# Output projection and MLP of a hybrid encoder layer: token blocks swapped in two tile sets, splits made in line, the mean square applied in mlp_down

## The chip, the core and the metric

The kernel runs on one core of one Trainium2 chip. The metric is the device time of one execution in microseconds (us). Five engines work side by side, each through its own instructions in order: TensorE (PE, matrix products), VectorE (DVE), ScalarE (ACT), GpSimd (POOL) and SyncE (SP, which here only issues transfers). On-chip tiles lie in SBUF; matrix products accumulate in PSUM, in eight tiles of 128 x 512 float32. Semaphores make an instruction wait for what it needs.

## What is computed

One layer over x (1, 2048, 1024) in float32: three token mixers (a chunkwise mLSTM, neighbourhood attention, attention into 256 memory tokens), a gated merge, an output projection into the residual stream, and an MLP. The part that the change touches is the end:

```python
def rmsnorm(x, g):
    xf = x.astype(jnp.float32)
    y = xf * lax.rsqrt(jnp.mean(xf * xf, axis=-1, keepdims=True) + EPS)
    return (y * g.astype(jnp.float32)).astype(x.dtype)
...
    y = (gates[:, :, 0] * (h_m @ w_proj_mlstm)
         + gates[:, :, 1] * (h_na @ w_proj_na)
         + gates[:, :, 2] * (h_mem @ w_proj_mem))
    x = x + y @ w_out

    u = rmsnorm(x, g_ffn) @ w_up
    return x + jnp.square(jax.nn.relu(u)) @ w_down
```

D_MODEL is 1024, D_FF is 4096. The norm's factor 1/sqrt(ms), with ms the mean square of a token plus EPS, goes through the relu, is squared to 1/ms, and so can be applied to the MLP's output: out = x + (1/ms) * (relu(x g w_up)^2 w_down).

## The kernel before

Phases 1 and 2 (norm, input projection, mixers) take the first 1300 us. Phase 3 works on token blocks of 512 in two pairs: blocks 3 and 2, then 1 and 0. In a pair, j = 0 is its first block and j = 1 its second. For each pair it runs merge, out_proj, 16 steps of mlp_up and mlp_down.

**Exact float32 products.** mm3 (L230) makes a product of three matmuls of 128 x 512: high part by high part, high by low, low by high (L235, L236, L237). So each operand is split: ACT copies it into a rounded type (the high part), and DVE subtracts that from the source (the low part).

**merge** writes the merged y of a block in both parts into eight 128 x 512 planes, yT[j]: for block 0 the tile hT, for block 1 the tiles b21 and t4, which both lie in the tile B.

**out_proj** takes w_out in two halves of four output tiles. Before, each half runs block 0's four tiles and then block 1's. A tile: load xC (L1354), 24 matmuls, DVE addition (L1363), store of the result x2 to memory, square on ACT (L1371) and its addition into the sum of squares gbc (L1372), and operands(), which makes the operands of the MLP: sums and differences of the four quarters (two blocks by two halves) as a seven-product scheme needs them, called b11, t1, b22, t2, t3, b21 and t4. less() subtracts both parts of an operand made earlier. Block 1's last quarter can't be split at once, since b21 and t4 are still being read as its yT planes: its four tiles are staged in half of uout (the tile that hT becomes after its last read), and eight jobs split them later, at ticks inside PE's sequence (L1400, L1403, L1411, L1412). inverse(), a job too, takes the mean over channels of gbc by a float32 matmul with ones (L1385), scales it (L1386) and takes the reciprocal (L1387), once for each block.

**mlp_up** is a step of seven products, 84 matmuls, for 256 of the 4096 channels. The sixth product reads b21, the seventh t4. The third goes into the PSUM tile c12, is copied by ACT (L1455), and the fifth accumulates into the same tile. The step squares the relu (L1471) and stores its sums. The up weights' seven operands are split on ACT and DVE by fetch_sums (L184) a step ahead.

**mlp_down** is four sweeps over the seven products; each product is 16 x 12 matmuls into four PSUM tiles. A ring of tiles (six places, in the first pair's last part four and then two, since the places go to the next pair's merge) takes operands loaded by SP (L1510 to L1517) and split by ACT and DVE (L1522, L1523). A product is summed into acc for one or two of four outputs (two blocks by two halves): the first by a copy on ACT (L1559), the next by DVE (L1561). Ahead of an output's last product x2 is loaded (L1535), acc is multiplied by 1/ms (L1537) and x2 added (L1538); behind it the product is multiplied (L1555) and added (L1556), and the result is stored.

**Order.** PE's sequence is that of the code (manual_schedule). The other engines' is set by a scheduler, by the priority at which an instruction is emitted; SOON, LATER and LATER_A shift it. ev() gives 128 x 512 tiles from a pool; an instruction into one waits until its last use is done.

**nsb.** In phase 2, na_scores takes a score tile of 128 x 480 from a pool of three and clears the columns behind the scores with a GpSimd memset (L1097).

Of the kernel before, what the change touches and what calls it, by code (L numbers as in the profile page):

```python
# [22 lines left out]
D = 1024  # L23
# [60 lines left out]
class Body:  # L84
# [995 lines left out]
    def na_scores(self, u, h):  # L1080
# [6 lines left out]
        sb = self.t("nsb", [128, 480], 3)  # L1087
# [5 lines left out]
        nc.vector.reciprocal(rs, sm)  # L1093
        nc.vector.tensor_scalar(sb[:, :nk], sb[:, :nk], rs, None, ALU.mult)
        kp = len(u["kts"]) * 120
        if kp > nk:
            nc.gpsimd.memset(sb[:, nk:kp], 0.0)  # L1097
        return u, h, sb

    def na_transpose(self, u, h, sb):  # L1100
# [166 lines left out]
    def phase_3(self):  # L1267
# [20 lines left out]
        for i in range(0, NB, 2):  # L1288
            pair = order[i:i + 2]
            if i:  # L1290
                self.hT = self.p_h.tile([128, 2, 8, TB], F32R, name="yT", tag="hT", bufs=1)
            yT = [[self.hT[:, l] for l in range(2)], [planes("b21"), planes("t4")]]
            self.ahead = 4
            self.merge(pair, mix, yT)
            self.out_proj(pair, yT, i)

            for q in range(FF // 256):
                self.mlp_up(i // 2, q)
            self.ahead = AHEAD
            self.mlp_down(i // 2, pair, [(b, m) for b, m in zip(order[i + 2:i + 4], mix)])  # L1300
# [36 lines left out]
    def out_proj(self, pair, yT, i):  # L1337

        nc, a = self.nc, self.a
        stage = None
        for half in range(2):
            ws = self.take(4)
            for j, b in enumerate(pair):
                if half and j:
                    self.up_tiles(i)
                    stage = self.uout[1].rearrange("p u i t -> p (u i) t")
                sq = self.gbc[:, j * TB:(j + 1) * TB]  # L1350
                for k, w in enumerate(ws):
                    c = 4 * half + k
                    x = self.ev()
                    nc.sync.dma_start(x, a["xC"][c, :, b * TB:(b + 1) * TB])  # L1354
                    p = self.ps("mm")
                    for n in range(8):
                        self.mm3(p, (w[:, 0, n], w[:, 1, n]), (yT[j][0][:, n], yT[j][1][:, n]), n == 0, n == 7)
                        if n % 2:
                            self.tick()
                    to = x if stage is None else stage[:, k]  # L1360
                    prio = self.tc.cur_priority
                    self.tc.cur_priority = prio - SOON
                    nc.vector.tensor_tensor(to, x, p, ALU.add)  # L1363
                    self.tc.cur_priority += SOON
                    x = to
                    self.store(self.scr["x2"][b][c], x)
                    if c == 0:
                        nc.scalar.activation(sq, x, AF.Square)
                    else:
                        e = self.ev()  # L1370
                        nc.scalar.activation(e, x, AF.Square)  # L1371
                        nc.vector.tensor_tensor(sq, sq, e, ALU.add)  # L1372
                    if stage is None:
                        self.operands(x, half, j, k)
                if half:
                    self.jobs += [None] * (LATER_3 - len(self.jobs) - 1) + [lambda sq=sq: self.inverse(sq)]
        for name in ("b21", "t4"):
            for k in range(4):
                self.jobs.append(lambda name=name, k=k, x=stage[:, k]: self.operands(x, 1, 1, k, name))

    def inverse(self, sq):

        nc = self.nc
        p = self.ps("mm")
        nc.tensor.matmul(p, self.ones, sq, start=True, stop=True)  # L1385
        nc.vector.tensor_scalar(sq, p, 1.0 / D, EPS, ALU.mult, ALU.add)  # L1386
        nc.vector.reciprocal(sq, sq)  # L1387

    def operands(self, x, half, j, k, late=None):
# [5 lines left out]
        f32 = lambda n, l: part(n, l).bitcast(F32)  # L1395

        def split(n, src, scale=None):
            if scale is None:
                nc.scalar.activation(part(n, 0), src, AF.Copy)
                nc.vector.tensor_tensor(part(n, 1), src, f32(n, 0), ALU.subtract)  # L1400
            else:
                nc.scalar.activation(part(n, 0), src, AF.Copy, scale=scale)
                nc.vector.scalar_tensor_tensor(part(n, 1), src, scale, f32(n, 0), ALU.mult, ALU.subtract)  # L1403

        def less(src, n, scale=None):

# [1 line left out]
            if scale is None:  # L1408
                nc.vector.tensor_tensor(e, src, f32(n, 0), ALU.subtract)
            else:  # L1410
                nc.vector.scalar_tensor_tensor(e, src, scale, f32(n, 0), ALU.mult, ALU.subtract)  # L1411
# [72 lines left out]
    def mlp_down(self, i, pair, then):  # L1484
# [43 lines left out]
        for q in range(0, FF // 256, 4):  # L1528
            for _, _, s, more, out in products:
                last = q == FF // 256 - 4 and (out, s, more) in ((0, 1, False), (3, 0, True), (1, 1, True), (2, 0, True))  # L1530
                if last:
                    j, h0 = pair[out // 2], out % 2 * 512
                    r2, xs = self.gbc[:, out // 2 * TB:(out // 2 + 1) * TB], [self.ev() for _ in range(4)]
                    for t, x in enumerate(xs):
                        nc.sync.dma_start(x, self.scr["x2"][j][out % 2 * 4 + t])  # L1535
                        c = acc[:, out, t]
                        nc.vector.tensor_tensor(c, c, r2, ALU.mult)  # L1537
                        nc.vector.tensor_tensor(x, x, c, ALU.add)  # L1538
                for dq in range(4):
                    if dq % 2 == 0:  # L1540
                        while todo and len(ready) < ring(total - len(todo))[1]:
# [9 lines left out]
                                 not more and dq == 0, dq == 3, more)  # L1551
                for t, p in enumerate(sets[s]):
                    c = acc[:, out, t]
                    if last:
                        nc.vector.tensor_tensor(c, p, r2, ALU.mult)  # L1555
                        nc.vector.tensor_tensor(xs[t], xs[t], c, ALU.add)  # L1556
                        self.store(self.a["out"][h0 + t * 128:h0 + t * 128 + 128, j * TB:(j + 1) * TB], xs[t])
                    elif out not in seen:
                        nc.scalar.activation(c, p, AF.Copy)  # L1559
                    else:  # L1560
                        nc.vector.tensor_tensor(c, c, p, ALU.add)  # L1561
                seen.add(out)

            sets.reverse()

# [74 lines left out]
```

## Time and profile before

| | us |
|---|---|
| median of 3 runs (2916.24 to 2921.32) | 2919.31 |
| profiled run, its own time | 2916.24 |
| its span | 2914.5 |
| merge, first and second pair | 87.05, 87.04 |
| out_proj | 88.88, 89.07 |
| 16 up steps | 317.97, 318.14 |
| mlp_down | 314.46, 304.79 |

The span is what the profiler sees of an execution; 1.74 us lie around it. The stage lengths are from PE's instructions of the trace: merge of the first pair from 1300.80 to 1387.85, of the second from 2109.16 to 2196.20; the others are in the rows quoted below. The mean granted clock is 0.993 of full speed. In a timeline a row gives start, length, engine, line, operation, output <- input, shape, and in brackets the idle time ahead of it and what ended it.

### The profile page before, as it was taken

Reading aid. Unit: us, or ns where it says so; the run is one execution under the profiler, and the core shown is the slowest. Engines: PE = TensorE matmul, PEld = TensorE weight load, DVE = VectorE, ACT = ScalarE, POOL = GpSimd, SP = SyncE. Lnnn points to the kernel's source line nnn. Section 1 sums busy time; section 2 is a strip of 40 time slices with the busy share of each in tenths; the row PEclk is TensorE's granted clock in tenths of the full one; section 3 lists DMA queues with packets and bytes.
Section 4 is the critical chain, followed back from the end, with each engine's and each line's share of the span. In section 5 each row is a group of like instructions: output and inputs, shape, how many; then the busy total and the mean of one; then the engine's idle time right before and its main releaser. Section 6 shows DMA issues by size and latency. Waiting matters only on the chain.

```text
span 2914.5 us, 41662 instructions
## 1 busy us (share of the span) xinstructions
PE 2862.8 (98%) x14932; PEld 2361.3 (81%) x14932; DVE 2055.8 (71%) x3494; ACT 1186.9 (41%) x2224; POOL 214.2 (7%) x382
## 2 busy tenths in 40 slices
PE   8999999999999999999989999999999899999999
PEld 6888788878878888888868888888788688888887
DVE  6676865477764556738688887666886888885668
ACT  6464654355543443532333334433223333344332
POOL 4121210021000122300000000000000000000000
PEclk9999999999999999999999999999999999999999
DMA  8786878877898788977344447556763344476554
GB/s 277 228 280 192 245 238 248 261 224 224 272 307 301 253 282 270 311 267 240 105 137 148 149 159 253 210 197 225 276 203 116 123 159 154 150 243 208 192 190 160
DMA packets 345151, 632.24 MB, mean 217 GB/s; under 512 B 29584, under 2 KB 151376, under 8 KB 344944
## 3 DMA queue, kind: packets, MB, share of 16 engines
q1 hardware_dynamic: 344944, 629.58, 66.2%
q8 instruction: 118, 1.93, 0.3%
q14 instruction: 89, 0.73, 0.1%
HBM read 452.85 MB, written 176.62 MB: 216 GB/s over the span
## 4 chain that ended last, share of the span: by engine, by line
PE 77%; DVE 9%; issue 8%; DMA 4%; ACT 1%; SPq 1%; POOL 0%; DVEq 0%; POOLq 0%; ACTq 0%
PE mm L235 24%; PE mm L237 23%; PE mm L236 23%; DMA wr<-in_w_units_dram 1%; PE tr L1105 1%; PE pn L882 1%; DVE ws L180 1%; DMA ev<-in_xC_dram 1%; PE pn L885 1%; PE mx L891 1%; PE mx L1119 1%; PE mx L1086 1%; DVE ev L1412 1%; DVE ev L1411 1%; DMA nak<-s_ks 1%
## 5 line engine op out<-in xcount | busy, mean ns | idle before, releaser
L235 PE MATMUL mm<-X,ws 128*128 128x512 f32 x896 | 352.8, 394 | 0.0
L236 PE MATMUL mm<-X,ws 128*128 128x512 f32 x896 | 351.0, 392 | 0.0
L237 PE MATMUL mm<-X,ws 128*128 128x512 f32 x896 | 350.6, 391 | 0.0
L180 DVE TENSOR_TENSOR ws<-wr,ws 128x1024 fp32r<-128x1024 f32 (+1 forms) x194 | 240.9, 1248 | 127.2 <-ACT ws L179 124.1
L235 PE MATMUL mm<-hT,ws 128*128 128x512 f32 (+1 forms) x776 | 308.9, 398 | 1.3 <-ACT ev L565 0.7
L237 PE MATMUL mm<-hT,ws 128*128 128x512 f32 (+1 forms) x776 | 302.9, 390 | 0.0
L236 PE MATMUL mm<-hT,ws 128*128 128x512 f32 (+1 forms) x776 | 302.5, 390 | 0.0
L179 ACT ACTIVATE ws<-wr 128x1024 fp32r<-128x1024 f32 (+1 forms) x194 | 204.2, 1058 | 116.5 <-PE mm L237 81.7
L237 PE MATMUL mm<-X 128*128 128x512 f32 x616 | 241.1, 391 | 4.8 <-DVE X L1523 4.8
L235 PE MATMUL mm<-X 128*128 128x512 f32 x616 | 241.0, 391 | 1.0 <-ACT X L1522 1.0
L236 PE MATMUL mm<-X 128*128 128x512 f32 x616 | 240.7, 391 | 0.0
L235 PE MATMUL mm<-ws,hT 128*128 128x512 f32 (+2 forms) x640 | 233.1, 364 | 2.9 <-ACT zif L529 2.2
L205 ACT ACTIVATE ws<-wr 128x512 fp32r<-128x512 f32 x224 | 134.5, 628 | 230.0 <-PE mm L237 151.3
L237 PE MATMUL mm<-ws,hT 128*128 128x512 f32 (+2 forms) x640 | 225.1, 352 | 2.0 <-DVE hT L438 2.0
L236 PE MATMUL mm<-ws,hT 128*128 128x512 f32 (+2 forms) x640 | 224.2, 350 | 0.0
L235 PEld LDWEIGHTS mm<-X,ws 128*128 128x128 f32 x896 | 169.8, 189 | 36.4 <-issue 0.8
L236 PEld LDWEIGHTS mm<-X,ws 128*128 128x128 f32 x896 | 169.6, 189 | 36.3 <-issue 1.0
L237 PEld LDWEIGHTS mm<-X,ws 128*128 128x128 f32 x896 | 169.4, 189 | 35.2
L1522 ACT ACTIVATE X<-X 128x1024 fp32r<-128x1024 f32 x109 | 115.7, 1062 | 194.1 <-DMA X<-s_s 93.1
L1523 DVE TENSOR_TENSOR X<-X 128x1024 fp32r<-128x1024 f32 x109 | 132.2, 1223 | 59.7 <-ACT X L1522 58.9
L235 PEld LDWEIGHTS mm<-hT,ws 128*128 128x128 f32 x776 | 146.4, 189 | 32.4 <-issue 4.3
L237 PEld LDWEIGHTS mm<-hT,ws 128*128 128x128 f32 x776 | 146.1, 188 | 31.3
(285 smaller groups left out, 5981.8 us busy)
## 6 DMA issues: line engine op xcount, KB each, us to landing
wr<-in_w_units_dram SPq DMA_DIRECT2D x290, 512.0 KB
s_s<-u SPq DMA_DIRECT2D x32, 1024.0 KB
s_g<-ev SPq DMA_DIRECT2D x96, 256.0 KB
ev<-s_g SPq DMA_DIRECT2D x96, 256.0 KB
s_a<-u SPq DMA_DIRECT2D x96, 256.0 KB
X<-s_s SPq DMA_DIRECT2D x45, 512.0 KB
nab<-in_rpb_dram SPq DMA_DIRECT2D x96, 220.0 KB
xt<-in_w_units_dram SPq DMA_DIRECT2D x32, 512.0 KB
```

The lines of the kernel that those rows point to most:

```text
L179: nc.scalar.activation(w[:, 0], raw, AF.Copy)
L180: nc.vector.tensor_tensor(w[:, 1], raw, w[:, 0].bitcast(F32), ALU.subtract)
L205: nc.scalar.activation(hi, src, AF.Copy)
L235: mm(out, lhs[0], rhs[0], start=first, stop=False)
L236: mm(out, lhs[0], rhs[1], start=False, stop=False)
L237: mm(out, lhs[1], rhs[0], start=False, stop=last)
L882: mm(pn[h % 2][:, h // 2], pt[:, h], v1[:, h], start=h < 2, stop=first)
L885: mm(pn[h % 2][:, h // 2], qw[hp, h // 2], C[hp, h // 2], start=False, stop=True)
L891: nc.tensor.matmul(pu[hp, h // 2], kw[:, h], v1[:, h], start=True, stop=True)
L1086: nc.tensor.matmul(psc[:, :nk], q[:, h, u["half"] * 128:u["half"] * 128 + 128], kl, start=True, stop=True)
L1522: nc.scalar.activation(hi, src, AF.Copy)
L1523: nc.vector.tensor_tensor(lo, src, hi.bitcast(F32), ALU.subtract)
```

## The change

- **Blocks swapped.** Block 0's yT planes are b21 and t4, block 1's are hT. In out_proj's first half the two blocks of a tile follow each other (k outside, j inside); in the second half all of block 0 comes first. So when block 1's last quarter comes, b21 and t4 are free, and its tiles are split at once; the staging and the eight late jobs go, and up_tiles (uout, utmp) is called behind out_proj.
- **t1** is the difference of the two blocks' first halves. Block 0's tile is kept (kept[k]) until block 1's comes, the difference is taken from the two and split once. Before it was made of block 0's operand through less(). 88 in place of 96 DVE operations on tiles in each pair.
- **inverse()** becomes means(), ahead of the third up step (q == 2): both blocks' matmuls with ones and the scaling, with no reciprocal. gbc then holds ms.
- **mlp_down** loads x2 at an output's first product, multiplies it by ms, and adds the first product to it (DVE, no ACT copy); then sums as before. At the last product acc is multiplied by 1/ms and stored. The reciprocals are taken in place in the first sweep, behind the last product that opens an output.
- **nsb**: three tiles cleared once; DVE clears the columns again only for units with g == 7, in which fewer key columns are filled.

```diff
+        self.nsb = [p_a.tile([128, 480], F32, name=f"nsb{i}") for i in range(3)]
+        for x in self.nsb:
+            nc.vector.memset(x, 0.0)
...
-        if kp > nk:
-            nc.gpsimd.memset(sb[:, nk:kp], 0.0)
+        if u["g"] == 7:
+            nc.vector.memset(sb[:, nk:kp], 0.0)
...
-            yT = [[self.hT[:, l] for l in range(2)], [planes("b21"), planes("t4")]]
+            yT = [[planes("b21"), planes("t4")], [self.hT[:, l] for l in range(2)]]
             self.ahead = 4
             self.merge(pair, mix, yT)
-            self.out_proj(pair, yT, i)
-
+            self.out_proj(pair, yT)
+            self.up_tiles(i)
             for q in range(FF // 256):
+                if q == 2:
+                    self.means()
                 self.mlp_up(i // 2, q)
...
         for half in range(2):
             ws = self.take(4)
+            for k, j in [(k, j) for k in range(4) for j in range(2)] if not half else [(k, j) for j in range(2) for k in range(4)]:
+                b, c, w = pair[j], 4 * half + k, ws[k]
...
+                self.operands(x, half, j, k, kept)
+
+    def means(self):
+
+        nc = self.nc
+        for j in range(2):
+            sq = self.gbc[:, j * TB:(j + 1) * TB]
+            p = self.ps("mm")
+            nc.tensor.matmul(p, self.ones, sq, start=True, stop=True)
+            nc.vector.tensor_scalar(sq, p, 1.0 / D, EPS, ALU.mult, ALU.add)
...
         if half == 0 and j == 0:
-
-            split("t1", x, g)
+            kept[k] = x
         elif half == 0:
             split("b11", x, g)
-            split("t1", less(x, "t1", g), -1.0)
+            e = self.ev()
+            nc.vector.tensor_tensor(e, kept.pop(k), x, ALU.subtract)
+            split("t1", e, g)
...
-        elif late == "b21":
+        else:
             split("b21", x, g)
-        else:
             split("t4", less(x, "t2", g))
...
+                r2 = self.gbc[:, out // 2 * TB:(out // 2 + 1) * TB]
+                first = [] if out in seen else [self.ev() for _ in range(4)]
+                for t, x in enumerate(first):
+                    nc.sync.dma_start(x, self.scr["x2"][j][out % 2 * 4 + t])
+                    nc.vector.tensor_tensor(x, x, r2, ALU.mult)
...
                     c = acc[:, out, t]
+                    nc.vector.tensor_tensor(c, first[t] if first else c, p, ALU.add)
                     if last:
-                        nc.vector.tensor_tensor(c, p, r2, ALU.mult)
-                        nc.vector.tensor_tensor(xs[t], xs[t], c, ALU.add)
...
-                    elif out not in seen:
-                        nc.scalar.activation(c, p, AF.Copy)
-                    else:
-                        nc.vector.tensor_tensor(c, c, p, ALU.add)
+                        x = self.ev()
+                        nc.vector.tensor_tensor(x, c, r2, ALU.mult)
...
                 seen.add(out)
+                if q == 0 and out == 2:
+                    for n in range(2):
+                        r2 = self.gbc[:, n * TB:(n + 1) * TB]
+                        nc.vector.reciprocal(r2, r2)
```

The lines of the changed kernel lie three lower in the MLP (L1523 before is L1520, L1450 is L1447, L1455 is L1452), and in out_proj L1403 is L1400, L1400 is L1397, L1411 and L1412 are L1408 and L1409.

How the instructions move on DVE, first at the end of the first pair's out_proj and the start of its first up step. A row is a line, an operation, output <- inputs and a shape; u is the tile that holds the staged tiles and the up step's results, B holds b21 and t4, X the other operands, ws and wr the up weights. Before:

```order
L1372 TENSOR_TENSOR gbc<-gbc,ev_16069 128x512
L212 TENSOR_TENSOR wr_16074<-wr_16072,wr_16074 128x512
L1403 SCALAR_TENSOR_TENSOR B<-u_15939,gffn,B 128x512
L213 TENSOR_TENSOR wr_16072<-wr_16074,wr_16072 128x512
L1411 SCALAR_TENSOR_TENSOR ev_16173<-u_15939,gffn,X 128x512
L217 TENSOR_TENSOR wr_16072<-wr_16072 128x512
L1386 TENSOR_SCALAR gbc<-mm_16127 128x512
L206 TENSOR_TENSOR ws_16076<-wr_16072,ws_16076 128x512
L1387 RECIPROCAL gbc<-gbc 128x512
L1412 TENSOR_TENSOR ev_16173<-ev_16173,X 128x512
L1411 SCALAR_TENSOR_TENSOR ev_16184<-u_15939,gffn,X 128x512
```

The same place in the changed kernel, from the third tile of block 1:

```order
L1363 TENSOR_TENSOR ev_15771<-ev_15771,mm_15773 128x512
L1397 TENSOR_TENSOR B<-ev_15766,B 128x512
L1408 SCALAR_TENSOR_TENSOR ev_15805<-ev_15771,gffn,X 128x512
L1372 TENSOR_TENSOR gbc<-gbc,ev_15800 128x512
L1400 SCALAR_TENSOR_TENSOR B<-ev_15771,gffn,B 128x512
L1409 TENSOR_TENSOR ev_15805<-ev_15805,X 128x512
L1363 TENSOR_TENSOR ev_15810<-ev_15810,mm_15812 128x512
L1397 TENSOR_TENSOR B<-ev_15805,B 128x512
L1408 SCALAR_TENSOR_TENSOR ev_15844<-ev_15810,gffn,X 128x512
L1372 TENSOR_TENSOR gbc<-gbc,ev_15839 128x512
L1400 SCALAR_TENSOR_TENSOR B<-ev_15810,gffn,B 128x512
```

Before, the weights' splits and inverse() stand between the last additions and t4's first split; now each tile's b21 and t4 splits follow its own addition, and no reciprocal is there.

On ACT at the same place, the changed kernel's last rows of out_proj and the copies of the first up step (L1452 of the first product, L1456 of the third, into the tile of which the fifth accumulates):

```order
L1399 ACTIVATE B<-ev_15771,gffn 128x512
L1452 ACTIVATE u_15849<-mm_15876 128x512
L1396 ACTIVATE B<-ev_15805 128x512
L205 ACTIVATE ws_15856<-wr_15852 128x512
L1371 ACTIVATE ev_15839<-ev_15810 128x512
L1399 ACTIVATE B<-ev_15810,gffn 128x512
L205 ACTIVATE ws_15856<-wr_15850 128x512
L1456 ACTIVATE u_15849<-mm_15878 128x512
L1396 ACTIVATE B<-ev_15844 128x512
```

The last tile's square (L1371) and split (L1399) and two splits of up weights stand ahead of the copy L1456.

On DVE in the first pair's first sweep of mlp_down, around the products that open the third output (acc is the sum, mm a PSUM tile, ev the x2 tiles). Now:

```order
L1520 TENSOR_TENSOR B<-B 128x1024 x2
L1533 TENSOR_TENSOR ev_18447<-ev_18447,gbc 128x512
L1549 TENSOR_TENSOR acc_17979<-ev_18239,mm_17984 128x512
L1549 TENSOR_TENSOR acc_17979<-ev_18240,mm_17985 128x512
L1549 TENSOR_TENSOR acc_17979<-ev_18241,mm_17986 128x512
L1520 TENSOR_TENSOR B<-B 128x1024
L1549 TENSOR_TENSOR acc_17979<-ev_18242,mm_17987 128x512
L1520 TENSOR_TENSOR X<-wr_18347,X 128x1024
L1520 TENSOR_TENSOR B<-B 128x1024
L1533 TENSOR_TENSOR ev_18448<-ev_18448,gbc 128x512
```

Where rows of a first sum stand now, DVE had none before (ACT made that copy); and the products x2 times ms (L1533) now stand among the ring's splits. Of the 16 in a pair, eight stand in the third and fourth up step and eight in this sweep; the second block's reciprocal (L1558) stands right behind them.

On DVE at the end of that pair's last sweep, before, ahead of the split of the X tile that PE waits for longest:

```order
L1555 TENSOR_TENSOR acc_18227<-mm_18230,gbc 128x512
L1555 TENSOR_TENSOR acc_18227<-mm_18231,gbc 128x512
L1556 TENSOR_TENSOR ev_19995<-ev_19995,acc_18227 128x512
L1556 TENSOR_TENSOR ev_19996<-ev_19996,acc_18227 128x512
L1538 TENSOR_TENSOR ev_20082<-ev_20082,acc_18227 128x512
L1538 TENSOR_TENSOR ev_20083<-ev_20083,acc_18227 128x512
L1538 TENSOR_TENSOR ev_20084<-ev_20084,acc_18227 128x512
L1538 TENSOR_TENSOR ev_20085<-ev_20085,acc_18227 128x512
L1523 TENSOR_TENSOR X<-X 128x1024
```

And now:

```order
L1549 TENSOR_TENSOR acc_17979<-acc_17979,mm_17986 128x512
L1549 TENSOR_TENSOR acc_17979<-acc_17979,mm_17987 128x512
L1552 TENSOR_TENSOR ev_19764<-acc_17979,gbc 128x512
L1552 TENSOR_TENSOR ev_19768<-acc_17979,gbc 128x512
L1520 TENSOR_TENSOR B<-B 128x1024
L1520 TENSOR_TENSOR X<-X 128x1024
L1549 TENSOR_TENSOR acc_17979<-acc_17979,mm_17980 128x512
L1520 TENSOR_TENSOR X<-X 128x1024
L1552 TENSOR_TENSOR ev_19833<-acc_17979,gbc 128x512
```

The X tile's split stood behind eight operations of one product and four of the next; now it stands behind one addition of the product before it.

More of the change, by code (lines that the diff above doesn't have):

```diff
@@ L1086, in na_scores @@
         nc.tensor.matmul(psc[:, :nk], q[:, h, u["half"] * 128:u["half"] * 128 + 128], kl, start=True, stop=True)
-        sb = self.t("nsb", [128, 480], 3)
+        self.nsb.append(self.nsb.pop(0))
+        sb = self.nsb[0]
         mx = self.small(1, "n")
@@ L1335, in merge, with out_proj @@
                 nc.vector.scalar_tensor_tensor(lo, acc, 0.5, hi.bitcast(F32), ALU.mult, ALU.subtract)
-    def out_proj(self, pair, yT, i):
+    def out_proj(self, pair, yT):
         nc, a = self.nc, self.a
-        stage = None
+        kept = {}
         for half in range(2):
             ws = self.take(4)
[L1346 to L1349, printed above, removed]
-                sq = self.gbc[:, j * TB:(j + 1) * TB]
[L1351 to L1368, printed above, removed]
-                    else:
[L1370 to L1379, printed above, removed]
@@ L1381, in inverse @@
-    def inverse(self, sq):
-        nc = self.nc
[L1384 to L1389, printed above, removed]
+            for k, j in [(k, j) for k in range(4) for j in range(2)] if not half else [(k, j) for j in range(2) for k in range(4)]:
+                b, c, w = pair[j], 4 * half + k, ws[k]
+                x = self.ev()
+                nc.sync.dma_start(x, a["xC"][c, :, b * TB:(b + 1) * TB])
+                p = self.ps("mm")
+                for n in range(8):
+                    self.mm3(p, (w[:, 0, n], w[:, 1, n]), (yT[j][0][:, n], yT[j][1][:, n]), n == 0, n == 7)
+                    if n % 2:
+                        self.tick()
+                prio = self.tc.cur_priority
+                self.tc.cur_priority = prio - SOON
+                nc.vector.tensor_tensor(x, x, p, ALU.add)
+                self.tc.cur_priority += SOON
+                self.store(self.scr["x2"][b][c], x)
+                sq = self.gbc[:, j * TB:(j + 1) * TB]
+                if c == 0:
+                    nc.scalar.activation(sq, x, AF.Square)
+                else:
+                    e = self.ev()
+                    nc.scalar.activation(e, x, AF.Square)
+                    nc.vector.tensor_tensor(sq, sq, e, ALU.add)
+                self.operands(x, half, j, k, kept)
@@ L1392, in operands @@
+    def means(self):
+        nc = self.nc
+        for j in range(2):
+            sq = self.gbc[:, j * TB:(j + 1) * TB]
+            p = self.ps("mm")
+            nc.tensor.matmul(p, self.ones, sq, start=True, stop=True)
+            nc.vector.tensor_scalar(sq, p, 1.0 / D, EPS, ALU.mult, ALU.add)
+    def operands(self, x, half, j, k, kept):
         nc, X = self.nc, self.X
@@ L1395, in operands @@
         f32 = lambda n, l: part(n, l).bitcast(F32)
+        stt = nc.vector.scalar_tensor_tensor
         def split(n, src, scale=None):
@@ L1402, in split @@
                 nc.scalar.activation(part(n, 0), src, AF.Copy, scale=scale)
-                nc.vector.scalar_tensor_tensor(part(n, 1), src, scale, f32(n, 0), ALU.mult, ALU.subtract)
+                stt(part(n, 1), src, scale, f32(n, 0), ALU.mult, ALU.subtract)
         def less(src, n, scale=None):
@@ L1410, in less @@
             else:
-                nc.vector.scalar_tensor_tensor(e, src, scale, f32(n, 0), ALU.mult, ALU.subtract)
+                stt(e, src, scale, f32(n, 0), ALU.mult, ALU.subtract)
             nc.vector.tensor_tensor(e, e, f32(n, 1), ALU.subtract)
@@ L1425, in operands @@
             split("t3", less(t2, "b11"))
-        elif late == "b21":
+        else:
             split("b21", x, g)
-        else:
             split("t4", less(x, "t2", g))
@@ L1530, in mlp_down @@
                 last = q == FF // 256 - 4 and (out, s, more) in ((0, 1, False), (3, 0, True), (1, 1, True), (2, 0, True))
[L1531 to L1538, printed above, removed]
+                j, h0 = pair[out // 2], out % 2 * 512
+                r2 = self.gbc[:, out // 2 * TB:(out // 2 + 1) * TB]
[3 more added lines that the diff above has]
+                    nc.vector.tensor_tensor(x, x, r2, ALU.mult)
                 for dq in range(4):
@@ L1553, in mlp_down @@
                     c = acc[:, out, t]
+                    nc.vector.tensor_tensor(c, first[t] if first else c, p, ALU.add)
                     if last:
-                        nc.vector.tensor_tensor(c, p, r2, ALU.mult)
-                        nc.vector.tensor_tensor(xs[t], xs[t], c, ALU.add)
-                        self.store(self.a["out"][h0 + t * 128:h0 + t * 128 + 128, j * TB:(j + 1) * TB], xs[t])
-                    elif out not in seen:
-                        nc.scalar.activation(c, p, AF.Copy)
-                    else:
-                        nc.vector.tensor_tensor(c, c, p, ALU.add)
+                        x = self.ev()
+                        nc.vector.tensor_tensor(x, c, r2, ALU.mult)
+                        self.store(self.a["out"][h0 + t * 128:h0 + t * 128 + 128, j * TB:(j + 1) * TB], x)
                 seen.add(out)
+                if q == 0 and out == 2:
+                    for n in range(2):
+                        r2 = self.gbc[:, n * TB:(n + 1) * TB]
+                        nc.vector.reciprocal(r2, r2)
             sets.reverse()
```

1 line of the change is left out of this document (added).

## The prediction

> **What bounds the kernel now.** I read the busy shares and the chain of waits first, then the stages' windows, PE's waits, and the timelines around the longest of them. Busy time of each engine, and the shares of the chain that ended last:
>
> ```profile
> PE 2862.8 (98%) x14932; PEld 2361.3 (81%) x14932; DVE 2055.8 (71%) x3494; ACT 1186.9 (41%) x2224; POOL 214.2 (7%) x382
> ```
> ```profile
> PE 77%; DVE 9%; issue 8%; DMA 4%; ACT 1%; SPq 1%; POOL 0%; DVEq 0%; POOLq 0%; ACTq 0%
> ```
>
> TensorE (PE) is busy 98% of the span and most of the chain, and the change leaves its projection and MLP matmuls in number as they are. So it can only win where PE stands or runs slowly. The windows of phase 3 (stretch, its length, then busy time and instructions of each engine, granted clock, DMA share, GB/s) show where:
>
> ```profile
> 1387.85:1476.73 88.88, 88.20 (x388) 72.41 (x386) 66.67 (x97) 33.58 (x52) 0.00 (x0) 1.00 0.36 108
> 1476.73:1794.70 317.97, 310.31 (x1347) 254.37 (x1346) 262.53 (x396) 104.78 (x169) 0.00 (x0) 0.99 0.47 160
> 1794.70:2109.16 314.46, 307.98 (x1345) 253.77 (x1344) 219.49 (x255) 122.27 (x125) 0.00 (x0) 0.99 0.69 236
> 2196.20:2285.27 89.07, 88.19 (x387) 72.39 (x386) 66.48 (x97) 33.77 (x52) 0.00 (x0) 1.00 0.35 107
> 2285.27:2603.41 318.14, 311.63 (x1347) 255.15 (x1346) 262.81 (x396) 106.74 (x171) 0.00 (x0) 0.98 0.47 162
> 2603.41:2908.20 304.79, 304.79 (x1345) 252.14 (x1343) 213.81 (x251) 114.73 (x119) 0.00 (x0) 1.00 0.58 198
> 1528.14:1547.18 19.04, 19.04 (x85) 15.77 (x84) 15.64 (x24) 6.00 (x10) 0.00 (x0) 1.00 0.45 153
> 1794.70:1870.86 76.16, 76.16 (x337) 63.09 (x336) 48.90 (x51) 40.04 (x46) 0.00 (x0) 1.00 0.74 257
> 2023.18:2099.00 75.82, 69.34 (x297) 56.26 (x296) 71.30 (x95) 25.66 (x25) 0.00 (x0) 0.97 0.83 284
> ```
>
> Rows 1 to 3 are out_proj, the 16 up steps and mlp_down of the first pair, rows 4 to 6 those of the second. Row 7 is one undisturbed up step: 84 matmuls in 19.04 us, 0.2267 each. At that rate out_proj's 384 take 87.04 and the 1344 of the up steps, or of mlp_down, 304.64. Beyond that the stages hold 1.84 + 2.03 (out_proj), 13.33 + 13.50 (up) and 9.82 + 0.15 (down): **40.5 us without the 0.15**, all that there is to win. PE's waits from 1387.85 to 2908.2 (total, times, longest) and its timeline name the causes:
>
> ```profile
> PE mm L1385 <- DVE gbc L1372: 10.8, 4, 4.8
> PE mm L237 <- DVE X L1523: 4.8, 1, 4.8
> PE mm L236 <- DVE B L1400: 3.2, 6, 0.7
> ```
> ```profile
> 1459.42 1.13 PE L1385 MATMUL mm<-gbc,ones 128*128 128x512 f32 x2 [0.68 <-DVE gbc L1372]
> 1459.98 0.80 PE L235 MATMUL mm<-B,ws 128*128 128x512 f32 x1
> 1460.61 0.40 PE L236 MATMUL mm<-B,ws 128*128 128x512 f32 x1
> ```
> ```profile
> 1507.61 0.63 PE L235 MATMUL mm<-X,ws 128*128 128x512 f32 x1
> 1508.03 0.63 PE L236 MATMUL mm<-X,ws 128*128 128x512 f32 x1
> ```
> ```profile
> 2096.30 0.79 PE L237 MATMUL mm<-X 128*128 128x512 f32 x1 [4.83 <-DVE X L1523]
> 2096.89 0.63 PE L235 MATMUL mm<-X 128*128 128x512 f32 x1
> 2097.32 0.63 PE L236 MATMUL mm<-X 128*128 128x512 f32 x1
> ```
>
> The mean-square matmul (L1385) waits for the sum of squares, the first up step's last products for the late splits of B (L1400), and the end of mlp_down for a tile's low part (L1523). Behind both clusters matmuls follow each other at 0.42 and 0.43 us: the waits also cost clock. DVE is late each time:
>
> ```profile
> 1437.72 0.68 DVE L1363 TENSOR_TENSOR ev<-ev,mm 128x512 f32<-128x512 f32 x1
> ...
> 1444.23 0.68 DVE L1363 TENSOR_TENSOR ev<-ev,mm 128x512 f32<-128x512 f32 x1
> ```
> ```profile
> 1491.29 3.34 DVE L1387 RECIPROCAL gbc<-gbc 128x512 f32<-128x512 f32 x1
> ```
>
> In out_proj's second half a tile of block 0 costs DVE nine operations, 1444.23 - 1437.72 = 6.51 us, while PE needs 24 x 0.2267 = 5.44. Two reciprocals of 3.3 us, one for each block, come into that backlog; the second, at 1491.29, stands ahead of the late splits.
>
> **Part 1: out_proj and the up steps.** inverse() goes; the second block's tiles are split in line. Deadlines, counted from out_proj's start: matmuls end at 87.04, the up step's products take 2.72 each, so its sixth (b21) asks for its last tile at 102.7 and its seventh (t4) at 105.4. DVE falls behind by 4 x 1.07 = 4.3 over block 0, and has six operations per tile of block 1, about 6/9 of 6.51 = 4.3, so it wins back 1.1 a tile. But loads hold it too (an xC load's issue on SP, and the addition that waited for it):
>
> ```profile
> 1475.53 0.43 SPq L1354 DMA_DIRECT2D ev<-in_xC_dram  x1
> ```
> ```profile
> 1479.92 0.69 DVE L1363 TENSOR_TENSOR u<-ev,mm 128x512 f32<-128x512 f32 x1 [1.64 <-DMA ev<-in_xC_dram]
> ```
>
> A tile of xC is added 4.39 after its issue, and SP issues it behind the store of the tile before, so additions follow at 5 to 5.5. I place the four at 79.5, 85, 90.4 and 95.8, the last low parts at 98 (b21) and 100.5 (t4), nearly 5 before they are asked for. What is late next: the copy of the third product (ACT, L1455 before) stands behind the last tile's square and split on ACT, which need the addition at 95.8; about 99.0. The fifth product, into the same PSUM tile, starts at 97.9: PE waits about 1.1 to 1.2 in each pair, 2.4 in all (bounds 0 and the 4.8 of the longest wait now, each pair).
>
> The mean-square matmuls stay. Rows 1459.42 to 1460.61 give a call 1.19 - 0.23 = 0.96, four calls 3.8; at the third up step their sums have long been ready. What means() and the first x2 tiles give DVE there, two scalings and eight products at 0.68 and a 3.34 reciprocal, is about 10 us in three steps, where DVE has 19.04 - 15.64 = 3.4 free in each: no wait, since the up weights are split a step ahead. Gain: 1.84 + 2.03 + 13.33 + 13.50 - 3.8 - 2.4 = **24.5**.
>
> By the Trainium skill, "TensorE: Matmul & The Clock Gate", section "HAM oscillation — how this bites in real kernels", PE falls to half rate after idle gaps over some 3.4 us. By that page the 1.2 us waits left here cost no clock and the sum stands. The trace agrees at 2096.30 but not at 1507.61, where no wait of the cluster is above 0.7: by that row, some 1.7 us more in each pair, 2890. I keep the sum, as one wait is no cluster.
>
> **Part 2: the end of mlp_down.** Before, a last product has 16 DVE operations (L1537, L1538, L1555, L1556, four each), now eight: 32 fewer in the last sweep, at 0.685 each 21.9 us, and DVE's 71.30 of 75.82 falls to about 49. The stalled tile's load, its copy on ACT and its low part on DVE:
>
> ```profile
> 2082.57 0.38 SPq L1512 DMA_DIRECT2D X<-s_t  x1
> ```
> ```profile
> 2089.63 1.06 ACT L1522 ACTIVATE X<-X 128x1024 fp32r<-128x1024 f32 x1 [6.08 <-DMA X<-s_t]
> ```
> ```profile
> 2095.02 1.22 DVE L1523 TENSOR_TENSOR X<-X 128x1024 fp32r<-128x1024 f32 x1
> ```
>
> It lands at 2089.63; ACT's 1.06 and DVE's 1.22 would end at 2091.91, but the split starts at 2095.02, behind final operations of other products. PE wanted it at 2096.30 - 4.83 = 2091.47. With a free DVE it is 0.4 late, and the shorter waits for ACT and for a B tile, about 1.6 together, may stay: 2 of 9.82 remain. Gain **7.8** (bounds 0 and 9.8). The second pair's last sweep has no ring of two and lost 0.15: nothing there.
>
> **Part 3: the first sweep pays.** The first accumulation goes from ACT to DVE, and half of the x2 products and a reciprocal come into the sweep. Groups of the first pair's mlp_down (count, busy us, mean ns, idle before):
>
> ```profile
> L1561 DVE TENSOR_TENSOR acc<-acc,mm 128x512 f32<-128x512 f32 x80 | 52.7, 684 | 28.4 <-PE mm L237 28.2
> ...
> L1537 DVE TENSOR_TENSOR acc<-acc,gbc 128x512 f32<-128x512 f32 x16 | 10.4, 686 | 0.0
> ```
> ```profile
> L1559 ACT ACTIVATE acc<-mm 128x512 f32<-128x512 f32 x16 | 8.2, 596 | 1.9 <-DMA s_s<-u 1.9
> ```
>
> An addition out of PSUM costs what one from SBUF does, 684 against 686 ns. So 16 + 8 operations and 3.34 for the reciprocal are 19.8: DVE goes from 48.90 to 68.7 of 76.16. That still fits, and six tiles of 5.44 are split ahead, 32.6 of cover. Taken as 0 (bounds 0 and all 19.8 in each pair; nearer to 0, since the up steps run at 82% without a wait).
>
> **Part 4: the nsb tiles.** 128 GpSimd memsets go, 3 + 16 DVE memsets come. GpSimd's group, with what ended its idle time:
>
> ```profile
> L1097 POOL MEMSET nsb<- 128x40 f32 x128 | 16.8, 133 | 583.9 <-PE tr L1105 573.6 <-DVE sm L1232 3.7 <-DVE sm L1093 3.3
> ```
>
> GpSimd waited 573.6 us for PE's transposes, not PE for it, and has 0% of the chain. 16 memsets on DVE are at most 16 x 0.68 = 11, and DVE holds 9% of the chain, so about 1: taken as 0.
>
> **Sum.** 24.5 + 7.8 = 32.3.
>
> ```profile
> span 2914.5 us, 41662 instructions
> ```
>
> The profiled run took 2916.24 (span 2914.5 plus 1.74), so 2883.9; the median of the runs, 2919.31, lies 3.07 above it, so **2887**.
>
> **Rivals.** (a) The end of mlp_down is set by the transfer: the X tile took 7.06 from issue to ACT, and its ring has only two places. For it: ACT waited 6.08 for that landing. Against: ACT had done its part at 2090.69, and the 4.3 from there to the split's start are DVE's alone. Nothing of Part 2 is won: 2895. (b) The change doesn't do what it says at the start of the MLP: the tiles are split in line, but on a DVE that keeps its backlog and an ACT behind it, and the stall moves from L1400 to the copy of the third product or to b21. For it: 66.67 of 88.88 were busy without a hurry, and the backlog sat in the second half. Half of the up steps' 26.8 stays: 2900. (c) Slower: in the first sweep DVE stands at the products x2 times mean square, whose loads SP issues among the ring's tiles. Eight such loads a pair fall into the sweep. The cover is the sweep's free 7.5 plus the ring's 32.6, 40 us, or 5 a load. At 4.39 a load (the xC row) nothing shows; at 7.06 (the X row) 16.5 are lost in each pair, 33 in all, and nothing is won: 2920. It turns slower from there: 8 a load is 64 - 40 = 24 a pair, 2935. Against: the loads are issued long before, half of them in the up steps, and several fly at once.
>
> **How the numbers follow.** Forecast (2879 to 2892) 0.64; (a) 0.12; (b) 0.13; (c) 0.11, half of it by its slower end. About 0.2%, 5.8 us, is what a measurement can tell from no change. Low end: all 40.5 won, 2878.8. High end 2905: it takes in (a), (b), and a first sweep that loses half of Part 3's bound in one pair (2897), and leaves out (c), where the whole bound lies. Faster 0.89, same 0.05, slower 0.06.
>
> **What would show it.** Right: no wait of PE for the sum of squares; waits for B's low parts gone; up windows near 306 with about 1 us ahead of L235 in the first step, released by ACT; the first pair's mlp_down near 307; DVE near 69 in its first sweep and 49 in its last. Wrong: PE waiting for DVE's splits (L1520 now) or DVE for x2 in the first sweep, a clock under 1 at the start of the up steps, or b21 and t4 still late.

## The result and the profile after

The changed kernel takes **2876.17 us** (median of 4 runs, 2875.75 to 2878.04), the kernel before 2917.77 beside it (4 runs, 2913.05 to 2921.32): a ratio of 0.986, 95% interval 0.9843 to 0.9877, 41.6 us. Twice more in later comparisons it came to 2879.89 (0.9866, 0.9852 to 0.9879) and 2879.04 (0.9871, 0.9854 to 0.9887). The forecast was 2887 with a range of 2878.8 to 2905: the direction and the order of the gain are right, the first measurement lies 2.6 us under the range, the two repeats inside it, and the gain is 4 to 9 us larger than the 32.3 that were forecast.

Busy time of each engine, and the shares of the chain that ended last, in the changed kernel's profile (span 2874.1):

```profile
PE 2844.5 (99%) x14932; PEld 2351.5 (82%) x14932; DVE 2041.2 (71%) x3497; ACT 1165.7 (41%) x2184; POOL 200.4 (7%) x254
```
```profile
PE 89%; DVE 4%; DMA 4%; issue 1%; ACT 1%; SPq 0%; POOL 0%; DVEq 0%; ACTq 0%; POOLq 0%
```

As many matmuls as before, and 89% of the chain in place of 77%. The stages of phase 3 (stretch, length, busy time and instructions of each engine, granted clock, DMA share, GB/s), then the first pair's first and last sweep of mlp_down:

```profile
1382.37:1469.41 87.04, 87.04 (x386) 72.10 (x384) 59.78 (x91) 31.62 (x49) 0.00 (x0) 1.00 0.38 113
1469.41:1775.79 306.38, 306.38 (x1350) 253.02 (x1349) 263.71 (x401) 103.99 (x169) 0.00 (x0) 1.00 0.48 166
1775.79:2082.57 306.78, 305.52 (x1345) 252.02 (x1344) 217.24 (x247) 113.97 (x109) 0.00 (x0) 1.00 0.70 238
2169.61:2256.65 87.04, 87.04 (x385) 72.07 (x384) 60.20 (x91) 31.64 (x49) 0.00 (x0) 1.00 0.37 114
2256.65:2563.03 306.38, 306.38 (x1349) 253.08 (x1348) 263.16 (x401) 105.14 (x170) 0.00 (x0) 1.00 0.48 166
2563.03:2867.67 304.64, 304.64 (x1345) 252.15 (x1343) 212.46 (x243) 107.31 (x103) 0.00 (x0) 1.00 0.57 198
1775.79:1851.95 76.16, 76.16 (x338) 63.06 (x337) 64.13 (x73) 33.31 (x33) 0.00 (x0) 1.00 0.83 281
2004.27:2080.43 76.16, 74.90 (x328) 61.07 (x327) 52.46 (x63) 25.38 (x24) 0.00 (x0) 1.00 0.77 263
```

Both out_proj stages are now at the undisturbed 87.04. The waits of PE from 1382 to the end (total, times, longest) are two, where there were six kinds:

```profile
PE mm L237 <- DVE B L1520: 0.7, 1, 0.7
PE mm L237 <- DVE X L1520: 0.5, 1, 0.5
```

| loss against undisturbed matmuls, us | before | forecast | after |
|---|---|---|---|
| out_proj, both pairs | 1.84 + 2.03 | 0 | 0 |
| up steps, both pairs | 13.33 + 13.50 | 3.1 each | 1.74 + 1.74 |
| mlp_down, both pairs | 9.82 + 0 | 2 + 0 | 2.14 + 0 |
| sum | 40.5 | 8.2 | 5.6 |

The 0.15 that the prediction reads in the second pair's mlp_down is no loss: its window ends with the end of the last matmul, that of after one step of 0.2267 behind the start of it, and from start to start both stages take 304.64. So phase 3 gained 34.9 us in the profiles. Its start, the first pair's merge, moved too, from 1300.81 to 1295.31: 5.5 us in phases 1 and 2. Together this is the 40.4 by which the spans differ.

The mean squares, on PE's timeline:

```profile
1507.49 1.88 PE L1381 MATMUL mm<-gbc,ones 128*128 128x512 f32 x4
1508.81 0.79 PE L235 MATMUL mm<-X,ws 128*128 128x512 f32 x1
1509.44 0.40 PE L236 MATMUL mm<-X,ws 128*128 128x512 f32 x1
```

PE waits for nothing there; the two calls cost 1509.44 - 1507.49 - 0.23 = 1.72 together, against 2 x 0.96 forecast, and this is all that the up steps lose.

### The profile page after: what moved, and what is told of

Same layout as the page of the kernel before. It is cut to its first block, busy times and chain, and to the rows that moved or that the text cites. A ratio compares the mean times of both kernels' runs of the same rounds, so it can differ in the third digit from the quotient of the medians.

```text
span 2874.1 us, 41423 instructions
## 1 busy us (share of the span) xinstructions
PE 2844.5 (99%) x14932; PEld 2351.5 (82%) x14932; DVE 2041.2 (71%) x3497; ACT 1165.7 (41%) x2184; POOL 200.4 (7%) x254
## 4 chain that ended last, share of the span: by engine, by line
PE 89%; DVE 4%; DMA 4%; issue 1%; ACT 1%; SPq 0%; POOL 0%; DVEq 0%; ACTq 0%; POOLq 0%
PE mm L235 28%; PE mm L237 27%; PE mm L236 27%; PE tr L1109 1%; DMA wr<-in_w_units_dram 1%; PE pn L885 1%; DVE ws L180 1%; PE mx L1089 1%; PE mx L1123 1%; PE pn L888 1%; PE mx L894 1%; PE mx L1262 0%; DMA s_t<-xt 0%; DVE cy L693 0%; PE mx L1233 0%
## 5 line engine op out<-in xcount | busy, mean ns | idle before, releaser
L237 PEld LDWEIGHTS mm<-X,ws 128*128 128x128 f32 x896 | 168.2, 188 | 34.9
L1549 DVE TENSOR_TENSOR acc<-acc,mm 128x512 f32<-128x512 f32 x192 | 126.1, 683 | 71.8 <-PE mm L237 71.7
```

The source lines that it names most:

```text
L237: mm(out, lhs[1], rhs[0], start=False, stop=last)
L1549: nc.vector.tensor_tensor(c, first[t] if first else c, p, ALU.add)
```

## The experiments

Each is the kernel before or the changed kernel with one edit. Times are medians, beside the kernel before on the same chip.

### Each half of Part 1 alone, and both together

**Swap and splits in line only** (out_proj and operands() of the change; inverse() early and with its reciprocals, mlp_down and nsb as before):

```diff
...
+                self.operands(x, half, j, k, kept)
+                if half and k == 3:
+                    self.jobs += [None] * (LATER_3 - len(self.jobs) - 1) + [lambda sq=sq: self.inverse(sq)]
...
```

> Swap and splits in line alone: inverse() keeps its early places and its reciprocals, mlp_down and nsb are as before. By the prediction's account (DVE's backlog holds both the late splits and the sum of squares): PE's waits for B's low parts go or shrink below 1 us in all, the wait of the second mean square stays at 3 to 5, since its sum is asked for 5.4 us into the up steps and the last tile is added at 8.8. Up loses 7 to 9 in place of 13.4: 9 to 12 us faster in all, ratio 0.9965. If the reciprocals alone were the cause, nothing is won: 1.000.

Measured: 2912.56 against 2918.45, ratio 0.9979 (0.9969 to 0.9989): 5.9 us, less than the 9 to 12 expected. The one wait of PE in the first pair's out_proj and up steps, for the second mean square, and its place on PE's timeline:

```profile
PE mm L1375 <- DVE gbc L1366: 8.7, 1, 8.7
```
```profile
1493.84 2.08 PE L1375 MATMUL mm<-gbc,ones 128*128 128x512 f32 x2 [8.74 <-DVE gbc L1366]
1494.92 1.42 PE L235 MATMUL mm<-X,ws 128*128 128x512 f32 x1
```

B's splits no longer hold PE at all, as expected, but the wait for the sum of squares grew from at most 4.8 to 8.7 (8.0 in the second pair), where 3 to 5 were expected: the additions now have their splits in line ahead of them. Up loses 12.8 and 11.2 us, not 7 to 9: in each pair nearly all of the loss has moved into one wait and the slow matmuls behind it.

**Only inverse() moves** (with its reciprocals, ahead of the third up step; late splits as before):

```diff
+                if q == 2:
+                    for j in range(2):
+                        self.inverse(self.gbc[:, j * TB:(j + 1) * TB])
                 self.mlp_up(i // 2, q)
...
-                if half:
-                    self.jobs += [None] * (LATER_3 - len(self.jobs) - 1) + [lambda sq=sq: self.inverse(sq)]
```

> Only inverse() moves, with its reciprocals, ahead of the third up step; staged splits, mlp_down and nsb are as before. The waits of the mean square go (5.4 us a pair), but PE then asks for b21 and t4 that much sooner, and DVE is only two reciprocals (6.7) ahead: by the prediction's account 4 to 6 us of waits for B's splits stay in a pair, with slow matmuls behind them; 8 to 14 us faster in all, ratio 0.9955 to 0.997. If the mean square alone were the cause: up near 306.5 a pair, 27 faster, 0.991.

Measured: 2909.44 against 2918.45, ratio 0.9969 (0.9956 to 0.9981): 9.0 us. Its largest wait in phase 3 (both pairs), and the place on PE's timeline:

```profile
PE mm L235 <- ACT B L1400: 14.6, 2, 7.3
```
```profile
1499.49 0.77 PE L235 MATMUL mm<-B,ws 128*128 128x512 f32 x1 [7.33 <-ACT B L1400]
1500.05 0.63 PE L236 MATMUL mm<-B,ws 128*128 128x512 f32 x1
1500.48 0.63 PE L237 MATMUL mm<-B,ws 128*128 128x512 f32 x1
```

Here the mean square holds nobody, both out_proj stages are at 87.04, and PE runs sooner into B's late splits: 7.3 us in each pair, where 4 to 6 were expected, and then matmuls at 0.43. Up loses 12.1 in each pair.

**Both together** (mlp_down and nsb as before):

> Swap and splits in line, and inverse() with its reciprocals ahead of the third up step: the two edits that won 5.9 and 9.0 us alone, together; mlp_down and nsb as before. If each hides the other's wait (the sum of squares behind the splits, the splits behind the mean square): out_proj at 87.04 and up at 306.4 in both pairs, 27 us faster, ratio 0.9905 to 0.9915. If they simply add up: 15 us, 0.995. The reciprocals at this place cost nothing, as DVE has 3.4 us free in a step and the weights are split ahead.

Measured: 2890.08 against 2915.38, ratio 0.9909 (0.9894 to 0.9924): 25.3 us, where the two alone give 14.9. Both out_proj stages take 87.04. Its up steps, first and second pair, and the one wait in them:

```profile
1473.66:1780.12 306.46, 306.46 (x1350) 252.93 (x1348) 262.47 (x394) 103.93 (x168) 0.00 (x0) 1.00 0.48 166
2269.24:2576.36 307.12, 306.69 (x1349) 252.93 (x1348) 263.36 (x396) 106.70 (x172) 0.00 (x0) 1.00 0.48 167
```
```profile
2280.71 0.50 PE L235 MATMUL mm<-X,ws 128*128 128x512 f32 x1 [0.43 <-ACT u L1452]
```

30.7 of loss became 4.3: 26.4 won. The two waits covered each other, and either edit alone exposes the other. The second pair loses 0.7 more than the first, and its one wait is that of the fifth product for ACT's copy of the third (L1452 here), not one behind the two reciprocals, which in this run stand at the third up step. They cost nothing that this profile shows: moving them on into mlp_down is not what wins the time.

### mlp_down alone

Only mlp_down changes; inverse() writes its reciprocal to a tile that nothing reads, so that its time stays:

```diff
-        nc.vector.reciprocal(sq, sq)
+        nc.vector.reciprocal(self.ev(), sq)
...
```

> Only mlp_down changes (x2 times mean square first, additions on DVE); inverse() keeps its place and its reciprocals' time, written to a tile that nothing reads. By the prediction: the first pair's mlp_down goes from 314.5 to 307, 7.7 us faster, ratio 0.9974, no wait in the first sweep. By the rival that the additions overload the first sweep: waits for L1520 there and 0 to 10 us a pair given back.

Measured: 2908.66 against 2918.45, ratio 0.9971 (0.9959 to 0.9983): 9.8 us. The first pair's mlp_down and its first sweep:

```profile
1793.44:2099.95 306.51, 305.24 (x1345) 252.10 (x1344) 217.44 (x248) 113.88 (x109) 0.00 (x0) 1.00 0.70 238
1793.44:1869.60 76.16, 76.16 (x337) 63.08 (x336) 64.46 (x74) 33.32 (x33) 0.00 (x0) 1.00 0.82 281
```

314.46 became 306.51, 8 us, and the first sweep stays at 76.16 with DVE at 64.5. The up steps are 1.1 and 1.4 us longer than before (their waits, for the sum of squares and for B's splits, are no longer than before), so phase 3 gives some 5.5 of the 9.8; 2.4 more lie ahead of merge in this profile, and the interval is 3.5 to each side.

### How much the first sweep can carry

Every addition of the first sweep is made four times; the output is then another:

```diff
                     nc.vector.tensor_tensor(c, first[t] if first else c, p, ALU.add)
+                    for _ in range(3 if q == 0 else 0):
+                        nc.vector.tensor_tensor(c, c, p, ALU.add)
```

> The changed kernel in which every addition of the first mlp_down sweep is made four times (84 more of about 0.60 us, 50 us in each pair; the output is then another). DVE is at 64 of 76 us in that sweep, so 38 us don't fit. If the six tiles split ahead (32.6 us) are the cover that the prediction took: mlp_down is 5 to 10 us longer in each pair. If there is no such cover: 38 longer in each pair. If the next sweep's slack takes it all: 0.

Measured: one run of 2932.3. mlp_down of the first and the second pair, and PE's largest wait from the first mlp_down on:

```profile
1776.12:2111.61 335.49, 317.25 (x1345) 257.35 (x1344) 265.16 (x331) 113.58 (x109) 0.00 (x0) 0.96 0.63 217
2592.07:2923.90 331.83, 314.79 (x1344) 255.83 (x1343) 260.97 (x327) 107.34 (x103) 0.00 (x0) 0.96 0.53 182
```
```profile
PE mm L235 <- DVE acc L1551: 33.8, 19, 4.5
```

28.7 and 27.2 us longer, between the two cases. All 19 waits are for a PSUM tile that DVE hasn't added yet (L1551 is the repeated addition); the ring's only waits are the two that the change has too, 0.7 and 0.5 near the end of the first pair's mlp_down. So the six tiles split ahead are not what covers an overload here. What fits is PSUM's two sets of four tiles, which let PE run one product ahead, 48 matmuls in a sweep or 10.9 us: 38 that don't fit less 10.9 is 27. That size is worked out from one run and not tested by itself. The change stays 12 us under the sweep's length and never comes to that.

### The nsb tiles, and phases 1 and 2

**nsb alone:** 

> The kernel before with the nsb edit alone. In the two profiles phase 3 gained 35 us and phases 1 and 2 (up to merge) 5.5, which the prediction had at nothing. Theory A, the GpSimd memsets or the pool's waits cost PE time in phase 2: 4 to 6 us faster than before (ratio 0.998 to 0.9985), and merge starts near 1295. Theory B, one execution of the first 1300 us differs from the next by that much (landing of transfers, granted clock) and the edit is worth nothing: ratio 1.000 within 0.001, merge's start anywhere from 1294 to 1302.

Measured: 2913.35 (12 runs) against 2916.57 (29 runs), ratio 0.9992 (0.9981 to 1.0003): 3.2 us, not told from none.

**All but nsb:** 

> The changed kernel with the nsb edit undone. Theory A: 35 us faster than before, ratio 0.988, merge starts near 1301. Theory B: as the whole change, ratio 0.986 to 0.988, merge's start anywhere from 1294 to 1302.

Measured: 2882.97 against 2916.57, ratio 0.9884 (0.9871 to 0.9898): 33.6 us. Its phase 3 is that of the change (out_proj 87.04 twice, up 306.38 and 306.96, mlp_down 307.45).

**Fixed tiles, GpSimd's memsets kept:** 

> The kernel before with three fixed nsb tiles, but GpSimd's 128 memsets kept. Theory A in the form that the memsets themselves cost (a fresh clear between a tile's last transpose and the next scores): ratio 1.000. In the form that the pool costs: 0.998. Theory B: 1.000 within 0.001.

Measured: 2915.06 against 2916.57, ratio 0.9993 (0.9984 to 1.0001).

**128 memsets on DVE:** 

> The kernel before with the 128 memsets on DVE in place of GpSimd, every time. If a memset beside the scores costs PE's path anything, 128 on the busier DVE cost more: up to 128 x 0.1 = 13 us slower, ratio 1.004. If DVE's slack hides them, 1.000.

Measured: 2923.38 against 2916.57, ratio 1.0025 (1.0017 to 1.0034), 6.8 us slower. In its profile one stretch of phase 2, 58 to 59 us long in all others, takes 69.9; PE waits there 5.4 for a load of attention keys and 3.4 for ACT. So 128 memsets on the busy DVE do cost; the change has 3 + 16.

Whole and all but nsb were then run once more, on one chip.

**The whole change, again:** 

> The changed kernel once more, beside the others, to set its distance to the run without the nsb edit (33.6 us faster than before). If nsb is worth 3 us, as alone: 36 to 38 faster than before, ratio 0.987 to 0.9875; if it is worth 6 to 7: 40 to 41, ratio 0.986.

Measured: 2879.89 against 2918.45, ratio 0.9866 (0.9852 to 0.9879): 38.6 us.

**The whole, a third time:** 

> The changed kernel, on the same chip as the next one, for the size of the nsb edit: 38 to 41 us faster than before.

**All but nsb, on that chip:** 

> The changed kernel without the nsb edit, again. If nsb is worth 3 to 5 us: that much slower than the run before it. If the earlier 5 to 7 came from the chip or from single executions: within 2 us of it.

Measured: 2879.04 (0.9871, 0.9854 to 0.9887) and 2879.89 (0.9875, 0.986 to 0.989). On one chip nsb made 0.9 us. Over all runs the whole change has a median of 2878.4 (12 runs), all but nsb 2881.9 (8 runs). The single values for nsb are 0.9, 3.2 and 3.5 us; no comparison on one chip tells them from none.

Part of what differs from run to run in phases 1 and 2 is visible at one place. PE's longest wait of phase 2, for loads of the attention's scores, between 860 and 890 us, in the kernel before, nsb alone, the change, and the second run of all but nsb:

```profile
PE mx L1086 <- DMA nak<-s_ks: 2.9, 1, 2.9
```
```profile
PE mx L1089 <- DMA nab<-in_rpb_dram: 3.4, 1, 3.4
```
```profile
PE mx L1089 <- DMA wr<-in_w_units_dram: 1.5, 1, 1.5
```
```profile
PE mx L1086 <- DMA nab<-in_rpb_dram: 4.1, 1, 4.1
```

The stretch around it, from the first of PE's matmuls on hT after 720 us to the next on ws, takes 186.1, 186.2, 182.9 and 188.9 us in these four, and 181.1 in the run with the fourfold additions, which has no such wait. Against that last one the wait of 1.5 costs 1.8, and those of 2.9 to 4.1 cost 5.0 to 7.8: once as a wait, and up to once more as slow matmuls behind it. With nsb as changed it was 3.4, 1.5, 2.0, 2.9 and 0; without, 2.1 to 4.1 in seven profiles; it was 3.8 with fixed tiles and GpSimd's memsets, and 1.2 with 128 memsets on DVE. The sets with and without GpSimd's memsets overlap; that these memsets make the loads late is possible, but no run shows by which way.

## Why the prediction was right, and where it was not

**What bounds the kernel:** right. All that was won in phase 3 came from the 40.5 us of waits and slow matmuls, and no matmul was saved. What failed is that this was "all that there is to win": see Part 4 and the range.

**Part 1:** right in its cause and its deadlines. The last three additions of the second block, t4's last low part, the copy of the third product, and the issue of the last xC load (out_proj starts at 1382.37):

```profile
1467.27 0.69 DVE L1363 TENSOR_TENSOR ev<-ev,mm 128x512 f32<-128x512 f32 x1 [0.48 <-DMA ev<-in_xC_dram]
...
1472.32 0.69 DVE L1363 TENSOR_TENSOR ev<-ev,mm 128x512 f32<-128x512 f32 x1 [1.04 <-DMA ev<-in_xC_dram]
...
1476.66 0.69 DVE L1363 TENSOR_TENSOR ev<-ev,mm 128x512 f32<-128x512 f32 x1 [0.52 <-DMA ev<-in_xC_dram]
...
1481.60 0.68 DVE L1397 TENSOR_TENSOR B<-ev,B 128x512 fp32r<-128x512 f32 x1
```
```profile
1479.12 0.58 ACT L1456 ACTIVATE u<-mm 128x512 f32<-128x512 f32 x1
```
```profile
1473.46 0.38 SPq L1355 DMA_DIRECT2D ev<-in_xC_dram  x1
```

The three stand at 84.9, 90.0 and 94.3, forecast 85, 90.4 and 95.8, each held by its xC load as forecast, and t4's last low part ends at 99.9 (forecast 100.5). But the last addition came 4.3 us after the one before it, where I gave each such step 5.4: it stands 3.2 behind the issue of its load, not the 4.39 of the row that the forecast went by. So ACT's copy ended at 97.3 and not at 99.0, and the fifth product starts at 97.9 without a wait. **This is the term that was mis-sized in phase 3:** "PE waits about 1.1 to 1.2 in each pair, 2.4 in all" is 0, its lower bound. The margin is 0.6 us, and the place was the right one to look at: the same wait of the fifth product for this copy does stand in the second pair of three other runs, 0.43 us in both halves of Part 1, 0.29 in the first run of all but nsb and 0.76 with inverse() alone moved. The mean squares came 0.4 cheaper.

The clock rule weighed there was not put to a test by the change, which has no such wait. Behind the three waits just named the matmuls start 0.34 and then 0.23 to 0.24 apart, not 0.42: a single short wait cost no clock there, as the prediction took it.

**Part 2:** right, 2.14 left for the 2 that were forecast: waits of 0.53 and 0.73, and 0.9 in the matmuls beside them. The X tile's copy on ACT and its split, and the B tile's split:

```profile
2068.57 1.06 ACT L1519 ACTIVATE X<-X 128x1024 fp32r<-128x1024 f32 x1 [3.97 <-DMA X<-s_t]
```
```profile
2069.66 1.23 DVE L1520 TENSOR_TENSOR X<-X 128x1024 fp32r<-128x1024 f32 x1 [1.26 <-ACT X L1519]
...
2074.40 1.22 DVE L1520 TENSOR_TENSOR B<-B 128x1024 fp32r<-128x1024 f32 x1
2075.54 0.69 DVE L1552 TENSOR_TENSOR ev<-acc,gbc 128x512 f32<-128x512 f32 x1
2076.14 1.22 DVE L1520 TENSOR_TENSOR B<-B 128x1024 fp32r<-128x1024 f32 x1
```

DVE waits for ACT and ACT for the transfer: the X tile's 0.5 us is now the transfer's, and rival (a), that the transfer set all of the stall, falls. The B tile's 0.7 is still DVE's own order.

**Part 3:** right in its value, 0, and near in its load (64.1 against 68.7 of 76.16, and 52.5 against 49 in the last sweep). Both misses have the same source in part: an operation behind another on DVE starts 0.60 us after it, as the rows at 2075.54 and 2076.14 show, where 0.685 was counted for each, so what comes and what goes is worth less; and 14 of the 16 first additions fall in the first sweep. Its cover was wrong: with the fourfold additions PE waited for PSUM tiles and not for the ring, and one product's 10.9 us fits, where 32.6 were named. By its own sum rival (c) would then decide sooner, at 7.5 + 10.9 = 18.4 in place of 40, or 2.3 a load; it didn't come, and DVE never waits for x2 in that sweep.

**Part 4 and the range: the step that failed.** The low end, "all 40.5 won, 2878.8", put all that lies ahead of merge at nothing, without a reason, and started from one median of three runs, 2919.31, which lies 3.07 above the profiled run. Against the changed kernel's profiled run of 2875.88 the forecast of 2887 is 11.1 too long: 3.07 are that start, 2.6 are phase 3, nearly all of it the copy's wait, and 5.5 are the earlier start of merge. The two later profiles of the same changed kernel have merge's first matmul at

```profile
1300.23 0.39 PE L235 MATMUL mm<-X,ws 128*128 128x512 f32 x1
```
```profile
1299.42 0.39 PE L235 MATMUL mm<-X,ws 128*128 128x512 f32 x1
```

where the first has it at 1295.31 and the kernel before at 1300.81. From there to the end of phase 3 the three take 1572.4, 1572.3 and 1573.3 us. So what was won in phase 3 came back each time, and most of the 5.5 us did not: that the first measurement fell under the range is in part the luck of those executions. Where most of it lay can be read from the granted clock. It is 1.00 in all of phases 1 and 2 of that first profile; in the kernel before it is 0.97 from 0 to 52 us and from 583 to 642, and 0.99 from 726 to 912, which by these rounded clocks is an estimated 5 us (52 x 0.03 + 59 x 0.03 + 186 x 0.01). In the two later profiles it is 0.94 between 860 and 890.

Whether Part 4's own 0 for nsb was wrong stays open: merge starts between 1295.3 and 1300.2 in the five profiles that have the edit, and between 1298.4 and 1303.5 in the seven that have neither it nor a part of it, and no comparison on one chip tells the two kernels apart. All 56 runs of the kernel before go from 2911.7 to 2924.2 with a median of 2916.9. From there the low end would have been 2876.4, and the 2878.4 of all 12 runs of the changed kernel lies above it.

**Rival (b)**, the stall that only moves, didn't come in the change, but it is what either half of Part 1 does alone.

## What to carry to other kernels

Where two late things wait for the same backlogged engine, one wait hides the other: list what is asked for next when a wait goes, since edits that win 6 and 9 us alone won 25 together here. Moving work of an engine to a stretch where it has slack was free while it fitted the stretch; beyond that PE waited at the nearest buffer, the PSUM tiles, and not at the ring of inputs. A forecast's range needs the run-to-run spread of the stages that the change doesn't touch, and its start more than three runs: the profiles of one kernel differed by 4.9 us ahead of the part that was changed.

## What the runs showed of the hardware

A wait of PE for loads between 860 and 890 us can cost nearly twice its length, the second half in matmuls at 0.42 to 0.43 us in place of 0.227. PE's timeline behind the wait of 3.72 us in the first run of all but nsb, and some 1.2 us behind that of 2.85, at 874.46, in the kernel before:

```profile
877.40 0.63 PE L235 MATMUL mm<-hT,ws 128*128 128x512 f32 x1
877.82 0.63 PE L236 MATMUL mm<-hT,ws 128*128 128x512 f32 x1
```
```profile
875.82 0.62 PE L237 MATMUL mm<-hT,ws 128*128 128x512 f32 x1
876.24 0.63 PE L235 MATMUL mm<-hT,ws 128*128 128x512 f32 x1
```

Behind the change's wait of 1.52 at the same place the next matmuls stand 0.23 apart. The Trainium skill, "TensorE: Matmul & The Clock Gate", section "HAM oscillation — how this bites in real kernels", speaks of gaps over some 3.4 us; 3.72 agrees, but slow matmuls followed 2.85 here too, so the figure can't be taken as a safe bound. The length of the wait alone doesn't decide it. In the kernel before, a wait of 1.61 for DVE is followed by them 1.8 us later, with a granted clock of 0.50 from 620 to 623 us; with mlp_down alone, one of 2.09 is not:

```profile
618.13 1.06 PE L1119 MATMUL mx<-npt,nav 120*32 120x128 f32 x26 [1.61 <-DVE npt L1110]
619.92 0.63 PE L237 MATMUL mm<-ws,hT 128*128 128x512 f32 x1
```
```profile
874.51 0.39 PE L1086 MATMUL mx<-nak,naq 96*128 96x320 f32 x1 [2.09 <-DMA wr<-in_w_units_dram]
874.74 0.39 PE L235 MATMUL mm<-hT,ws 128*128 128x512 f32 x1
```

Transposes and small products of the attention stand around these waits; whether they count as idle, no run here separates.
